# A two-layer hybrid trunk in split float32: 512-column moving operands in the second MLP, rotary tables and low parts moved to GpSimd in the first layer

## The chip, the core and the metric

The kernel runs on one core of a Trainium2 chip. The metric is device time in microseconds (us) of one execution. In the profile PE is TensorE (PEld its weight load), DVE is VectorE, ACT is ScalarE, POOL is GpSimd, and SP issues most of the DMAs. PEclk is the TensorE clock that was granted, as a share of full speed: 1.00 is 2.4 GHz, 0.50 is 1.2 GHz.

## The reference, cut to what matters

Sequence 256, model width 2048, 2 layers, all float32. The widths are: combined input projection 7184 columns, output projection 2048, MLP 8192. `adaLN` takes six vectors per layer from a product of the condition with a 2048 x 12288 matrix.

```python
cond = jax.nn.silu(c)
for layer in range(DEPTH):
    mod = (cond @ ada_w[layer] + ada_b[layer])[:, None, :]
    sh_a, sc_a, g_a, sh_m, sc_m, g_m = jnp.split(mod, N_MOD, axis=-1)
    h = rmsnorm(x, norm_mix_w[layer]) * (1.0 + sc_a) + sh_a
    x = x + g_a * hybrid_mixer(h, ..., w_in[layer], ..., w_out[layer])
    h = rmsnorm(x, norm_mlp_w[layer]) * (1.0 + sc_m) + sh_m
    x = x + g_m * (jnp.square(jax.nn.relu(h @ w_ff1[layer])) @ w_ff2[layer])
return rmsnorm(x, final_norm_w)
```

`hybrid_mixer` projects h, runs three mixers on column groups of the result (4 retention heads with rotary positions, 8 forgetting-attention heads, 4 mLSTM heads behind a short causal convolution), normalises each head, gates, and projects the concatenation with `w_out`.

## The kernel before

**Number format.** Every large product is done with both operands split into a high part (fp32r) and a low part (the fp32r rest). A weight block of 128 x 128 and an activation tile of 128 x 256 (features x positions) give three matmuls that add into the same PSUM region: high weight x low activation, low weight x high activation, high weight x high activation (`mm_b`, lines 253 to 255). Where the result is wanted with positions on the partitions, the activations are the stationary side and 512 weight columns move (`mm_a`, lines 264 to 266).

**Weights.** A chunk of 512 KB is loaded by SP into a `raw` buffer (6 of them), `split` (line 217) rounds it to the high part `wh` on ACT (line 222) and subtracts on DVE or POOL to get the low part `wl` (line 228). There are 3 buffers each of `wh` and `wl`. A chunk holds 8 blocks of 128 x 128: 2 tiles of the inner dimension x 512 columns. `pool_share` accumulates, and each time it reaches 1 the subtraction goes to POOL, else to DVE: in layer 0 it is 1.0 for the first groups of the input projection, 0.8 for the last, 0.5 for the two late blocks, 0.7 to 0.8 after that; in layer 1 it is 0.

**Order of a layer.** The input projection runs over 14 blocks of 512 columns (`BLOCKS`), in layer 0 in groups of the inner dimension (`win`, 2, 2, 2, 4 and 6 tiles of 128) because the adaLN vectors arrive in that order, with blocks `mo` and `rg` last; in layer 1 in one group. When a mixer's inputs are there, `mixers` (line 838) makes it a generator, and `tick` (line 826), called between chunks, advances up to two generators by one step. A step is a few small matmuls, the ACT and DVE work that follows, and a `yield`. Then comes `w_out`, which needs the mixers' outputs `Y`, then the MLP: `ff1` (line 965) and `ff2` (line 1002), in 8 stages of 1024 hidden features; `residual` (line 817) adds each `ff2` result to X with one DVE instruction per 128 x 256 tile (line 822). PSUM for all of these is `pj`: 2 buffers of 128 x 1024, each 4 output tiles.

**Lead.** Layer 1's input projection and both MLPs begin with `lead` (line 468): the first block is computed from X with the scale applied but without the row norm R, while R is still being worked out; `h_make` (line 510) then makes the normed h (`hh`, `hl`) for the rest, two tiles at a time: one DVE multiply (518), two ACT scalings (523), an ACT cast (525), a DVE subtraction (526).

**Adaptive vectors.** `ada` (line 269) streams the 2048 x 12288 matrices in 512 KB halves, reduced on DVE (line 284), spread over the whole program by `pump` and `rate`.

**Rotary tables.** `rope_tables` (line 176) computes cosine and sine of position x frequency with 20 small DVE instructions, most of them a range reduction, and three ACT ones. It is called from `late_constants` (line 153) after the third group of layer 0's input projection (`CONST_AT = 2`).

The Tile framework's scheduler, which simulates a timeline while it builds, fixes the order of instructions on each engine.

## Time and profile before

| | |
|---|---|
| median of 3 runs | 2540.33 us (2539.73 to 2541.04) |
| the profiled execution: its own time | 2544.26 us |
| its span, first to last instruction | 2542.5 us |
| PE busy | 2440.4 us |
| DVE, ACT, POOL busy | 1583.5, 1186.6, 758.0 us |
| mean granted TensorE clock | 0.982 |

How to read it: the span is the profiled execution's first to last instruction; the execution's own time is 1.8 us more. The matmuls are pipelined, so the duration of one (about 0.28 us) overlaps the next; how often they start is read by dividing a stretch by the number of them in it.

### The profile page before, as it was taken

Reading aid. Unit: us, or ns where it says so; the run is one execution under the profiler, and the core shown is the slowest. Engines: PE = TensorE matmul, PEld = TensorE weight load, DVE = VectorE, ACT = ScalarE, POOL = GpSimd, SP = SyncE. Lnnn points to the kernel's source line nnn. Section 1 sums busy time; section 2 is a strip of 40 time slices with the busy share of each in tenths; the row PEclk is TensorE's granted clock in tenths of the full one; section 3 lists DMA queues with packets and bytes.
Section 4 is the critical chain, followed back from the end, with each engine's and each line's share of the span. In section 5 each row is a group of like instructions: output and inputs, shape, how many; then the busy total and the mean of one; then the engine's idle time right before and its main releaser. Section 6 shows DMA issues by size and latency. Waiting matters only on the chain.

```text
span 2542.5 us, 46522 instructions
## 1 busy us (share of the span) xinstructions
PE 2440.4 (96%) x19016; PEld 2368.9 (93%) x19016; DVE 1583.5 (62%) x2426; ACT 1186.6 (47%) x1446; POOL 758.0 (30%) x315
## 2 busy tenths in 40 slices
PE   7999988888999999999999999999999999999997
PEld 6989977888999999999998999889999999999997
DVE  5787877677664544544388778556754554555554
ACT  4434454435543444444446456454644444344443
POOL 4867533344676666666500000000000000000000
PEclk8999999899999999999999999999999999999998
DMA  9988867589999988888667777555555555555552
GB/s 355 341 294 314 307 215 273 207 312 339 334 333 331 329 303 305 289 299 315 222 230 268 259 255 265 157 167 179 179 182 183 185 186 182 186 187 185 185 183 99
DMA packets 177247, 630.45 MB, mean 248 GB/s; under 512 B 19588, under 2 KB 24326, under 8 KB 177032
## 3 DMA queue, kind: packets, MB, share of 16 engines
q1 hardware_dynamic: 176600, 627.08, 70.9%
q8 instruction: 149, 2.44, 0.4%
q14 instruction: 66, 0.54, 0.1%
q10 hardware_dynamic: 432, 0.39, 0.1%
HBM read 625.30 MB, written 2.10 MB: 247 GB/s over the span
## 4 chain that ended last, share of the span: by engine, by line
PE 78%; DVE 7%; issue 5%; POOL 4%; DMA 4%; ACT 2%; SPq 0%; DVEq 0%; POOLq 0%; ACTq 0%
PE pj L254 22%; PE pj L253 22%; PE pj L255 22%; POOL wl L228 4%; DMA ada<-ada_w 3%; DVE wl L228 2%; PE pj L265 2%; PE pj L264 2%; PE pj L266 2%; DVE ada L284 1%; DMA raw<-w_in 1%; PE mx L646 1%; DVE blk L453 0%; PE mx L430 0%; DVE X L822 0%
## 5 line engine op out<-in xcount | busy, mean ns | idle before, releaser
L222 ACT CAST wh<-raw 128x1024 fp32r<-128x1024 f32 x804 | 840.5, 1047 | 1117.2 <-PE pj L255 898.6
L228 DVE TENSOR_TENSOR wl<-raw,wh 128x1024 fp32r<-128x1024 f32 x494 | 615.5, 1248 | 504.5 <-ACT wh L222 504.1
L228 POOL TENSOR_TENSOR wl<-raw,wh 128x1024 fp32r<-128x1024 f32 (+1 forms) x310 | 755.4, 2441 | 501.7 <-ACT wh L222 474.8
L253 PE MATMUL pj<-hl,wh 128*128 128x256 f32 x2912 | 828.7, 285 | 14.2 <-DVE hl L526 9.8
L254 PE MATMUL pj<-hh,wl 128*128 128x256 f32 x2912 | 829.2, 285 | 4.5 <-DVE wl L228 4.0
L255 PE MATMUL pj<-hh,wh 128*128 128x256 f32 x2912 | 826.9, 284 | 0.0
L254 PE MATMUL pj<-blk,wl 128*128 128x256 f32 x2528 | 713.8, 282 | 7.9 <-DVE wl L228 7.0
L253 PE MATMUL pj<-blk,wh 128*128 128x256 f32 x2528 | 711.6, 282 | 1.5 <-ACT blk L564 1.5
L255 PE MATMUL pj<-blk,wh 128*128 128x256 f32 x2528 | 711.8, 282 | 0.0
L253 PEld LDWEIGHTS pj<-hl,wh 128*128 128x128 f32 x2912 | 559.6, 192 | 16.4 <-DVE hl L526 10.5
L254 PEld LDWEIGHTS pj<-hh,wl 128*128 128x128 f32 x2912 | 560.1, 192 | 6.6 <-DVE wl L228 5.4
L255 PEld LDWEIGHTS pj<-hh,wh 128*128 128x128 f32 x2912 | 560.0, 192 | 0.2
L284 DVE SCALAR_TENSOR_TENSOR ada<-ada,cond 128x1024 f32<-128x1024 f32 x380 | 456.5, 1214 | 165.0 <-DMA ada<-ada_w 162.5
L254 PEld LDWEIGHTS pj<-blk,wl 128*128 128x128 f32 x2528 | 478.1, 189 | 9.0 <-DVE wl L228 7.6
L253 PEld LDWEIGHTS pj<-blk,wh 128*128 128x128 f32 x2528 | 478.5, 189 | 1.9 <-ACT blk L564 1.9
L255 PEld LDWEIGHTS pj<-blk,wh 128*128 128x128 f32 x2528 | 478.7, 189 | 0.1
L1075 POOL TENSOR_TENSOR blk<-blk,R 128x1024 f32<-128x1024 f32 x1 | 2.4, 2362 | 1276.2 <-ACT R L420 1276.2
L822 DVE SCALAR_TENSOR_TENSOR X<-pj,mod,X 128x256 f32<-128x256 f32 x284 | 117.9, 477 | 103.5 <-PE pj L255 103.3
L265 PE MATMUL pj<-wl,hh 128*128 128x512 f32 x384 | 154.0, 401 | 13.6 <-DVE wl L228 12.5
L264 PE MATMUL pj<-wh,hl 128*128 128x512 f32 x384 | 153.2, 399 | 1.0 <-ACT wh L222 1.0
L266 PE MATMUL pj<-wh,hh 128*128 128x512 f32 x384 | 152.0, 396 | 0.0
L265 PEld LDWEIGHTS pj<-wl,hh 128*128 128x128 f32 x384 | 73.2, 191 | 29.7 <-DVE wl L228 14.1
(232 smaller groups left out, 1642.5 us busy)
## 6 DMA issues: line engine op xcount, KB each, us to landing
raw<-w_ff SPq DMA_DIRECT2D x508, 512.0 KB, 4.0
ada<-ada_w SPq DMA_DIRECT2D x380, 512.0 KB, 6.4
raw<-w_in SPq DMA_DIRECT2D x224, 512.0 KB, 5.3
raw<-w_out SPq DMA_DIRECT2D x64, 512.0 KB, 4.4
X<-x SPq DMA_DIRECT2D x4, 512.0 KB, 7.1
raw<-ada_w SPq DMA_DIRECT2D x4, 512.0 KB, 9.8
raw<-w_ff SPq DMA_DIRECT2D x8, 256.0 KB, 3.3
out<-blk SPq DMA_DIRECT2D x4, 512.0 KB, 2.8
```

Source lines behind the costliest of these rows:

```text
L222: nc.scalar.copy(hi, raw)
L228: eng.tensor_tensor(lo, raw, hi.bitcast(F32), ALU.subtract)
L253: nc.tensor.matmul(o, lhsT=wh[:, s], rhs=al, start=st, stop=False, skip_group_check=True)
L254: nc.tensor.matmul(o, lhsT=wl[:, s], rhs=ah, start=False, stop=False, skip_group_check=True)
L255: nc.tensor.matmul(o, lhsT=wh[:, s], rhs=ah, start=False, stop=last, skip_group_check=True)
L264: nc.tensor.matmul(o, lhsT=al[:, s], rhs=wh, start=first, stop=False)
L265: nc.tensor.matmul(o, lhsT=ah[:, s], rhs=wl, start=False, stop=False)
L266: nc.tensor.matmul(o, lhsT=ah[:, s], rhs=wh, start=False, stop=last)
L284: nc.vector.scalar_tensor_tensor(raw, raw, 1.0, self.cond, ALU.mult, ALU.mult, accum_out=self.part[l][:, i, h:h + 1])
L646: nc.tensor.matmul(ps[:, i * P:i * P + P], lhsT=lt, rhs=v[:, j, c:c + P], start=first, stop=last, skip_group_check=True)
L822: V.scalar_tensor_tensor(self.X(k), ps[:, n * T:n * T + T], self.mod[l][:, c:c + 1], self.X(k), ALU.mult, ALU.add)
L1075: nc.gpsimd.tensor_tensor(o, o, self.R[:, None, :].to_broadcast((P, 4, T)), ALU.mult)
```

## The change

In layer 1's MLP the activation tiles lie as high part beside low part (one tile `h` in place of `hh` and `hl`), and `mm_w` does one matmul of 512 columns, high weight x [high | low], and one of 256, low weight x high. The two halves of the 512 columns land beside each other in PSUM and are added when they are read: `ff1_wide` by an ACT copy and a DVE add, `ff2_wide` by two DVE residual instructions per tile. A `pj` buffer holds 2 output tiles in place of 4, and a weight chunk is 4 inner tiles x 256 columns (`chunk2`), laid out so in memory. `square_wide` does the squared ReLU as one DVE instruction. The lead of that MLP keeps three matmuls per block, and takes its weights from two such chunks at a time (`lead_w2`). The last four output tiles (`ff2_tail`) are unchanged but for the layout.

In layer 1 a generator may take a step only on every second call of `tick` (`gap=2`). In layer 0 the rotary tables are computed on POOL at the start of the program, each fused multiply-add as two instructions (29 in place of 20 on DVE), with their two DMAs on ACT's queue; the other late constants come after the first group (`CONST_AT = 0`); all weight low parts up to `w_out` go to POOL; and the transposed attention probabilities are copied from PSUM by ACT in place of DVE.

```diff
-CFG = [dict(win=[2, 2, 2, 4, 6], late=2, lead_win=False, ada_win=[4, 4, 8, 12, 14], ada_late=4, ada_out=19,
+CFG = [dict(wide=False, gap=1, win=[2, 2, 2, 4, 6], late=2, lead_win=False, ada_win=[4, 4, 8, 12, 14], ada_late=4, ada_out=19,
             ff1=[8, 8], ff1_blocks=6, early_ff1=[[0, 1]], stat_ff1=(0, 1), ada_ff1=[16, 16], ada_ff=68,
-            pool_win=[1.0, 1.0, 1.0, 1.0, 0.8], pool_late=0.5, pool_out=0.7, pool_ff1=[0.7, 0.8], pool_ff=0.8),
-       dict(win=[16], late=0, lead_win=True, ada_win=[36], ada_late=0, ada_out=12, early_win=[[0, 1, 2], [], [3]],
+            pool_win=[1.0, 1.0, 1.0, 1.0, 1.0], pool_late=1.0, pool_out=0.7, pool_ff1=[0.7, 0.8], pool_ff=0.8),
+       dict(wide=True, gap=2, win=[16], late=0, lead_win=True, ada_win=[36], ada_late=0, ada_out=12, early_win=[[0, 1, 2], [], [3]],
             stat_win=(1, 2), ff1=[16], ff1_blocks=1, early_ff1=[[0, 1], [2], [], [], [3]], stat_ff1=(1, 2),
             ada_ff1=[4], ada_ff=12, pool_win=[0.0], pool_late=0.0, pool_out=0.0, pool_ff1=[0.0], pool_ff=0.0)]
...
-CONST_AT = 2
+CONST_AT = 0
...
-        self.hh = self.acts.tile([P, KT, T], F32R, name="hh")
-        self.hl = self.acts.tile([P, KT, T], F32R, name="hl")
+        self.h = self.acts.tile([P, KT, 2, T], F32R, name="h")
...
-            self.rope_tables()
...
+        m = self.tmp.tile([P, 2, T], F32, tag="ht", name="rm")[:, 0, :]
+        nc.scalar.dma_start(pi.bitcast(I32), self.io["positions"].partition_broadcast(P))
         rope = c.tile([P, 2], F32, name="rope")
-        nc.sync.dma_start(rope, self.io["rope"])
-        V = nc.vector
+        nc.scalar.dma_start(rope, self.io["rope"])
+        V = nc.gpsimd
...
             for cc in (c1, c2, c3):
                 for p in parts:
-                    V.scalar_tensor_tensor(a, p, -cc, a, ALU.mult, ALU.add)
+                    V.tensor_scalar(m, p, -cc, None, ALU.mult)
+                    V.tensor_tensor(a, m, a, ALU.add)
...
+    def chunk2(self, src):
+        raw = self.raw.tile([P, 4, 256], F32, tag="raw", name=self.name("raw"))
+        self.wdma.append(self.nc.sync.dma_start(raw, src))
+        hi, lo = self.split(raw, 4, 256)
+        return [(hi[:, i, :], lo[:, i, :]) for i in range(4)]
+    def mm_w(self, ps, w, act, first, last):
+        nc = self.nc
+        wh, wl = w
+        for n in range(2):
+            s = slice(n * P, n * P + P)
+            o = ps[:, n * 512:n * 512 + 512]
+            nc.tensor.matmul(o.rearrange("p (a b) -> p a b", b=T), lhsT=wh[:, s], rhs=act, start=first, stop=False,
+                             skip_group_check=True)
+            nc.tensor.matmul(o[:, :T], lhsT=wl[:, s], rhs=act[:, 0, :], start=False, stop=last, skip_group_check=True)
+    @staticmethod
+    def sums(ps):
+        v = ps.rearrange("p (n c) -> p n c", c=512)
+        return v[:, :, 0:T], v[:, :, T:2 * T]
 
...
-                (wh, wl), (uh, ul) = w[k - k0], self.U.pop(k)
+                uh, ul = self.U.pop(k)
                 f, e = k == kts[0], k == kts[-1]
                 for n in range(4):
-                    s = slice(n * P, n * P + P)
+                    wh, wl = w(k - k0, n)
                     o = ps[n][:, :LT]
-                    nc.tensor.matmul(o, lhsT=wh[:, s], rhs=ul, start=f, stop=False)
-                    nc.tensor.matmul(o, lhsT=wl[:, s], rhs=uh, start=False, stop=False)
-                    nc.tensor.matmul(o, lhsT=wh[:, s], rhs=uh, start=False, stop=e)
+                    nc.tensor.matmul(o, lhsT=wh, rhs=ul, start=f, stop=False)
+                    nc.tensor.matmul(o, lhsT=wl, rhs=uh, start=False, stop=False)
+                    nc.tensor.matmul(o, lhsT=wh, rhs=uh, start=False, stop=e)
...
+    def lead_w2(self, src):
+        def get(k, nk):
+            w = [self.chunk2(src[b, k // 4]) for b in range(2)]
+            return lambda i, n: tuple(x[:, n % 2 * P:n % 2 * P + P] for x in w[n // 2][i])
+        return get
 
...
-            nc.scalar.copy(self.hh[:, k:k + 2, :], t)
-            nc.vector.tensor_tensor(self.hl[:, k:k + 2, :], t, self.hh[:, k:k + 2, :].bitcast(F32), ALU.subtract)
+            hi, lo = self.h[:, k:k + 2, 0, :], self.h[:, k:k + 2, 1, :]
+            nc.scalar.copy(hi, t)
+            nc.vector.tensor_tensor(lo, t, hi.bitcast(F32), ALU.subtract)
 
...
-            V.tensor_copy(p, ps[:, 0:384])
+            (V.tensor_copy if l else nc.scalar.copy)(p, ps[:, 0:384])
...
+        self.ticks += 1
         n = 0
         for t in list(self.tasks):
             if n == LANES:
                 break
-            r = next(t, None)
+            if t[1] > self.ticks:
+                continue
+            r = next(t[0], None)
             if r is None:
                 self.tasks.remove(t)
-            else:
-                n += r
+            elif r:
+                n += 1
+                t[1] = self.ticks + self.gap
 
...
+                if cfg["wide"]:
+                    self.lead_out(ps, acc[0])
+                    acc[0] = self.square_wide(acc[0])
...
+    def ff1_wide(self, l, b, kts, acc=None):
+        nc = self.nc
+        done = kts[-1] == KT - 1
+        fresh = acc is None
+        t = self.slot() if fresh else acc
+        for h in range(2):
+            ps = self.pair()
+            for k0 in range(kts[0], kts[-1] + 1, 4):
+                w = self.chunk2(self.io["w_ff1_%d" % l][2 * b + h, k0 // 4])
+                for k in range(k0, k0 + 4):
+                    self.mm_w(ps, w[k - k0], self.h[:, k], k == kts[0], k == kts[-1])
+                self.step(0.5)
+            d = t[:, 2 * h:2 * h + 2, :]
+            p0, p1 = self.sums(ps)
+            if fresh:
+                nc.scalar.copy(d, p1)
+            else:
+                nc.vector.tensor_tensor(d, p1, d, ALU.add)
+            nc.vector.tensor_tensor(d, p0, d, ALU.add)
+        return self.square_wide(t) if done else t
+    def square_wide(self, t):
+        nc = self.nc
+        nc.vector.scalar_tensor_tensor(t, t, 0.0, t, ALU.max, ALU.mult)
+        out = []
+        for h in range(2):
+            s = self.slot((P, 2, 2, T), F32R)
+            nc.scalar.copy(s[:, 0], t[:, 2 * h:2 * h + 2, :])
+            nc.vector.tensor_tensor(s[:, 1], t[:, 2 * h:2 * h + 2, :], s[:, 0].bitcast(F32), ALU.subtract)
+            out.append(s)
+        return lambda i: out[i // 2][:, :, i % 2, :]
+    def ff2_wide(self, l, s, hid, last):
+        V = self.nc.vector
+        if last:
+            self.stat_begin()
+            self.per = 0.0
+        tail = last and l == DEPTH - 1
+        for nb in range(6 if tail else 8):
+            ps = self.pair()
+            for c in range(2):
+                w = self.chunk2(self.io["w_ff2_%d" % l][nb, 2 * s + c])
+                for i in range(4):
+                    self.mm_w(ps, w[i], hid[c](i), c == 0 and i == 0, c == 1 and i == 3)
+                self.step(0.5)
+            for n in range(2):
+                k = 2 * nb + n
+                g = self.mod[l][:, 5 * KT + k:5 * KT + k + 1]
+                with self.tc.high_priority(offset=URGENT * last):
+                    for c in range(n * 512, n * 512 + 512, T):
+                        V.scalar_tensor_tensor(self.X(k), ps[:, c:c + T], g, self.X(k), ALU.mult, ALU.add)
...
         self.constants()
+        self.rope_tables()
         self.stat_first()
...
+    for k in ("w_ff1", "w_ff2"):
+        for l in range(DEPTH):
+            a[f"{k}_{l}"] = _chunks(inp[k][l:l + 1], 256 if CFG[l]["wide"] else 512)[0]
```

**Order, first place.** PE near the end of layer 0's mixers; `mx` are the mixers' PSUM banks, `pj` the output projection, `pt` the decayed retention scores. Lines 635 and 636 (675 and 676 in the change) are the scores of one head, line 646 (686) their product with the values, which needs `pt` from DVE (L715, L716). Before:

```order
L254 MATMUL pj_4300<-blk_3619,wl_4379 128x256
L255 MATMUL pj_4300<-blk_3619,wh_4378 128x256
L635 MATMUL mx_3969<-blk_531,blk_564 128x256
L636 MATMUL mx_3969<-blk_531,blk_564 128x128
L646 MATMUL mx_3969<-blk_596,pt_3972 128x128 x3
L635 MATMUL mx_4015<-blk_531,blk_564 128x256
L636 MATMUL mx_4015<-blk_531,blk_564 128x128
L646 MATMUL mx_4015<-blk_596,pt_4018 128x128 x3
```

And in the change, for the head that corresponds to the first of these:

```order
L675 MATMUL mx_3978<-blk_569,blk_602 128x256
L676 MATMUL mx_3978<-blk_569,blk_602 128x128
L278 MATMUL pj_4309<-blk_3195,wh_4318 128x256
L279 MATMUL pj_4309<-blk_3194,wl_4319 128x256
L280 MATMUL pj_4309<-blk_3194,wh_4318 128x256
```

Before, a head's scores and its product stand side by side for three heads in a row; now 27 matmuls of `w_out` stand between the two.

**Order, second place.** DVE in the middle of layer 1's `ff2`. L822 (L1124 in the change) is the residual, which waits for the last matmul of its `pj` buffer and frees it; L228 the low part of a weight chunk. Before:

```order
L822 SCALAR_TENSOR_TENSOR X_91<-pj_22204,mod_127,X_91 128x256 x4
L228 TENSOR_TENSOR wl_22393<-raw_22390,wh_22392 128x1024
L228 TENSOR_TENSOR wl_22399<-raw_22396,wh_22398 128x1024
L228 TENSOR_TENSOR wl_22458<-raw_22455,wh_22457 128x1024
L228 TENSOR_TENSOR wl_22464<-raw_22461,wh_22463 128x1024
L822 SCALAR_TENSOR_TENSOR X_92<-pj_22329,mod_127,X_92 128x256 x4
```

And in the change:

```order
L1124 SCALAR_TENSOR_TENSOR X_91<-pj_20098,mod_126,X_91 128x256 x3
L228 TENSOR_TENSOR wl_20200<-raw_20197,wh_20199 128x1024
L1124 SCALAR_TENSOR_TENSOR X_91<-pj_20098,mod_126,X_91 128x256
L228 TENSOR_TENSOR wl_20222<-raw_20219,wh_20221 128x1024
L1124 SCALAR_TENSOR_TENSOR X_92<-pj_20147,mod_126,X_92 128x256 x3
L228 TENSOR_TENSOR wl_20249<-raw_20246,wh_20248 128x1024
L1124 SCALAR_TENSOR_TENSOR X_92<-pj_20147,mod_126,X_92 128x256
```

Four residual instructions came with every four low parts, and now come with every two. The low parts between them belong to the buffer after the next one.

**Order, third place.** POOL at the start of the program; `rt` and `rm` are the rotary tables' scratch tiles. Before, after its set-up:

```order
L228 ISA
L228 TENSOR_TENSOR wl_214<-raw_211,wh_213 128x1024
L228 TENSOR_TENSOR wl_247<-raw_244,wh_246 128x1024
L228 TENSOR_TENSOR wl_280<-raw_277,wh_279 128x1024
L228 TENSOR_TENSOR wl_307<-raw_304,wh_306 128x1024
```

And in the change, where 15 rotary instructions stand ahead of this piece:

```order
L202 TENSOR_TENSOR rt<-rm,rt 128x256
L201 TENSOR_SCALAR rm<-rt 128x256
L228 TENSOR_TENSOR wl_252<-raw_249,wh_251 128x1024
L202 TENSOR_TENSOR rt<-rm,rt 128x256
L228 TENSOR_TENSOR wl_285<-raw_282,wh_284 128x1024
L228 TENSOR_TENSOR wl_318<-raw_315,wh_317 128x1024
L192 TENSOR_SCALAR rt<-rt 128x256
L193 TENSOR_SCALAR rt<-rt 128x256
```

The first low part is now behind 17 rotary instructions, the fourth behind 25.

## Rows read from the trace of the kernel before

**Rows 1.** The page: busy time of each engine, and the chain that ended last.

```profile
PE 2440.4 (96%) x19016; PEld 2368.9 (93%) x19016; DVE 1583.5 (62%) x2426; ACT 1186.6 (47%) x1446; POOL 758.0 (30%) x315
...
PE 78%; DVE 7%; issue 5%; POOL 4%; DMA 4%; ACT 2%; SPq 0%; DVEq 0%; POOLq 0%; ACTq 0%
```

**Rows 2.** Windows: stretch and its length, then busy time (instructions) of each engine.

```profile
core 0: us, PE busy (x) PEld busy (x) DVE busy (x) ACT busy (x) POOL busy (x), PEclk, DMA share, GB/s
...
1900.00:2500.00 600.00, 600.00 (x5047) 600.00 (x5046) 317.09 (x340) 256.33 (x252) 0.00 (x0) 1.00 0.56 185
...
1614.00:1640.00 26.00, 26.00 (x116) 21.51 (x115) 11.19 (x13) 16.37 (x22) 0.00 (x0) 1.00 0.61 183
...
137.00:177.00 40.00, 33.69 (x228) 30.97 (x227) 37.63 (x51) 13.79 (x18) 24.03 (x11) 0.96 0.73 245
...
340.00:470.00 130.00, 104.27 (x562) 88.43 (x561) 89.91 (x204) 66.23 (x114) 36.28 (x15) 0.88 0.59 211
...
413.40:423.60 10.20, 6.62 (x22) 5.27 (x20) 10.20 (x12) 2.95 (x4) 2.97 (x1) 0.50 0.51 161
447.50:468.00 20.50, 12.71 (x53) 11.14 (x52) 10.75 (x56) 11.48 (x25) 0.00 (x0) 0.50 0.00 0
```

**Rows 3.** Waits of PE from 340 to 470 us: total us, times, longest.

```profile
PE pj L265 <- DVE wl L228: 9.2, 4, 3.6
PE mx L646 <- DVE pt L716: 4.7, 3, 2.9
PE mx L807 <- DVE blk L799: 4.6, 1, 4.6
...
PE pj L253 <- ACT blk L564: 1.5, 1, 1.5
```

**Rows 4.** Groups of instructions from 1840 to 2500 us (layer 1's MLP), DVE and ACT.

```profile
L228 DVE TENSOR_TENSOR wl<-raw,wh 128x1024 fp32r<-128x1024 f32 x232 | 284.0, 1224 | 297.5 <-ACT wh L222 297.5
...
L822 DVE SCALAR_TENSOR_TENSOR X<-pj,mod,X 128x256 f32<-128x256 f32 x120 | 49.8, 478 | 15.8 <-PE pj L255 15.8
...
L222 ACT CAST wh<-raw 128x1024 fp32r<-128x1024 f32 x231 | 242.2, 1048 | 349.1 <-PE pj L255 337.9 <-DVE wl L228 10.7 <-ACT wh L222 0.5
```

**Rows 5.** Timeline of DVE at a residual: start, us, instruction, idle before and releaser.

```profile
1785.88 1.66 DVE L822 SCALAR_TENSOR_TENSOR X<-pj,mod,X 128x256 f32<-128x256 f32 x4 [0.56 <-PE pj L255]
```

**Rows 6.** Groups on ACT, 1803 to 1831 us, and PE's wait there (from 1700).

```profile
L523 ACT ACTIVATE ht<-ht,mod 128x256 f32<-128x256 f32 x16 | 8.7, 593 | 1.6 <-DVE ht L518 1.6
L525 ACT CAST hh<-ht 128x512 fp32r<-128x512 f32 x8 | 4.9, 615 | 0.1
...
PE pj L253 <- DVE hl L526: 1.4, 1, 1.4
```

**Rows 7.** One rotary line on DVE (ns min/median/max), and PE's waits, 137 to 180 us.

```profile
L193 DVE TENSOR_SCALAR rt<-rt x2: 293/1043/1793, 141.5 to 158.0; 128x256 f32<-128x256 f32 x2
...
PE mx L294 <- DVE ada L284: 2.6, 2, 2.1
PE pj L253 <- DVE blk L567: 2.3, 1, 2.3
```

**Rows 8.** Groups from 340 to 470 us (low parts), and the convolution's line over the program.

```profile
L228 POOL TENSOR_TENSOR wl<-raw,wh 128x1024 fp32r<-128x1024 f32 x15 | 38.0, 2535 | 94.7 <-ACT wh L222 94.7
...
L228 DVE TENSOR_TENSOR wl<-raw,wh 128x1024 fp32r<-128x1024 f32 x11 | 20.2, 1845 | 0.5 <-ACT wh L222 0.5
...
L735 DVE SCALAR_TENSOR_TENSOR cv<-blk,vec,cv x48: 433/478/2701, 299.2 to 1574.6; 128x255 f32<-128x255 f32 x16, 128x254 f32<-128x254 f32 x16, 128x253 f32<-128x253 f32 x16
```

**Rows 9.** Waits of PE in layer 1's input projection, 1380 to 1700 us.

```profile
PE pj L265 <- DVE wl L228: 3.2, 1, 3.2
PE mx L646 <- DVE pt L687: 1.5, 1, 1.5
```

**Rows 10.** Timeline at the start: POOL's first low part, PE's first weight matmul.

```profile
24.04 2.35 POOL L228 TENSOR_TENSOR wl<-raw,wh 128x1024 fp32r<-128x1024 f32 x1 [23.60 <-ACT wh L222]
...
32.18 0.58 PE L253 MATMUL pj<-hl,wh 128*128 128x256 f32 x1 [6.67 <-DVE hl L526]
```

More of the change, by code (lines that the diff above doesn't have):

```diff
@@ L479, in lead @@
             nk = min(4, kts[-1] + 1 - k0)
-            w = self.chunk(wsrc(k0, nk), nk)
+            w = wsrc(k0, nk)
             for k in range(k0, k0 + nk):
@@ L496, in lead, with lead_w, get @@
         return ps
+    def lead_w(self, src):
+        def get(k, nk):
+            w = self.chunk(src[0, k // 4][:, k % 4:k % 4 + nk, :], nk)
+            return lambda i, n: tuple(x[:, n * P:n * P + P] for x in w[i])
+        return get
+    def lead_w2(self, src):
+        def get(k, nk):
+            w = [self.chunk2(src[b, k // 4]) for b in range(2)]
+            return lambda i, n: tuple(x[:, n % 2 * P:n % 2 * P + P] for x in w[n // 2][i])
+        return get
     def lead_out(self, ps, dst, func=AF.Identity, scale=1.0):
@@ L842, in mixers @@
             g = int(nm[2])
[L843 removed]
+            self.tasks.append([self.fox(l, B.pop("fq%d" % g), B.pop("fk%d" % g), B.pop("fv%d" % g), g), 0])
         elif nm == "mq":
@@ L862, in layer @@
         io = self.io
-        self.state, self.Y, self.tasks = {}, {}, []
+        self.state, self.Y, self.tasks, self.ticks, self.gap = {}, {}, [], 0, cfg["gap"]
         G = self.groups(cfg["win"])
@@ L870, in layer @@
             if led:
-                ps = self.lead(l, 0, 1, lambda k, n: io["w_in"][l, 0, k // 4][:, k % 4:k % 4 + n, :], kts, cfg["stat_win"])
+                ps = self.lead(l, 0, 1, self.lead_w(io["w_in"][l]), kts, cfg["stat_win"])
             if l > 0:
@@ L930, in layer @@
         NST = 8
+        ff1, ff2 = (self.ff1_wide, self.ff2_wide) if cfg["wide"] else (self.ff1, self.ff2)
         hid = [None] * NST
@@ L940, in layer @@
             if led:
-                ps = self.lead(l, 3, 4, lambda k, n: io["w_ff1"][l, 0, k // 4][:, k % 4:k % 4 + n, :], kts, cfg["stat_ff1"])
+                ps = self.lead(l, 3, 4, (self.lead_w2 if cfg["wide"] else self.lead_w)(io["w_ff1_%d" % l]), kts, cfg["stat_ff1"])
             self.h_make(l, 3, 4, kts)
@@ L950, in layer @@
             for b in range(1 if led else 0, nb):
-                acc[b] = self.ff1(l, b, kts, acc.get(b))
+                acc[b] = ff1(l, b, kts, acc.get(b))
         self.pool_share = cfg["pool_ff"]
@@ L955, in layer @@
             if s < NST:
-                hid[s] = [acc.pop(2 * s + i) if 2 * s + i < nb else self.ff1(l, 2 * s + i, list(range(KT)))
+                hid[s] = [acc.pop(2 * s + i) if 2 * s + i < nb else ff1(l, 2 * s + i, list(range(KT)))
                           for i in range(2)]
@@ L959, in layer @@
                 self.pump_until(l, 5, KT - 1)
-                self.ff2(l, s - 1, hid[s - 1], s == NST)
+                ff2(l, s - 1, hid[s - 1], s == NST)
                 hid[s - 1] = None
@@ L970, in ff1 @@
             r0 = k0 % 4
-            w = self.chunk(self.io["w_ff1"][l, b, k0 // 4][:, r0:r0 + nk, :], nk)
+            w = self.chunk(self.io["w_ff1_%d" % l][b, k0 // 4][:, r0:r0 + nk, :], nk)
             for i in range(nk):
@@ L1006, in ff2 @@
             self.per = 0.0
-        tail = last and l == DEPTH - 1
-        for nb in range(3 if tail else 4):
+        for nb in range(4):
             ps = self.pair()
@@ L1012, in ff2 @@
                     self.early(CFG[l + 1]["early_win"], c, l + 1, 0, 1)
-                w = self.chunk(self.io["w_ff2"][l, nb, 2 * s + c], 4)
+                w = self.chunk(self.io["w_ff2_%d" % l][nb, 2 * s + c], 4)
                 hi, lo = hid[c]
@@ new lines, in square_wide @@
+    def square_wide(self, t):
[27 more added lines that the diff above has]
+                        V.scalar_tensor_tensor(self.X(k), ps[:, c:c + T], g, self.X(k), ALU.mult, ALU.add)
+            if last and nb % 2 == 1:
+                self.stat_piece(nb // 2)
@@ L1024, in ff2 @@
             if tail:
-                for n in range(4):
-                    self.final_scale(4 * nb + n)
+                for n in range(2):
+                    self.final_scale(2 * nb + n)
         if tail:
@@ L1113, in _layout @@
     a["w_gate"] = np.ascontiguousarray(g.reshape(DEPTH, KT, P, NG).transpose(0, 2, 1, 3))
-    for k in ("w_out", "w_ff1", "w_ff2"):
-        a[k] = _chunks(inp[k])
+    a["w_out"] = _chunks(inp["w_out"])
+    for k in ("w_ff1", "w_ff2"):
+        for l in range(DEPTH):
+            a[f"{k}_{l}"] = _chunks(inp[k][l:l + 1], 256 if CFG[l]["wide"] else 512)[0]
     vec = np.zeros((P, DEPTH * NVEC + KT), np.float32)
```

24 lines of the change are left out of this document (11 added, 13 removed).

## The prediction, made before the change was run

> **What bounds the kernel now.** I read the page first [rows 1]: PE is busy 96% of the span and carries 78% of the chain that ended last, while DVE is at 62%. So only two things shorten the program: PE doing its work in fewer or shorter intervals, and the 4% in which PE waits or its clock is low. I then went through windows [rows 2]. Most of the MLPs look like 1900 to 2500 us: PE is never idle and the clock is at 1.00. What PE loses sits in a few stretches of layer 0: 137 to 177 us has 40 − 33.7 = 6.3 us idle, 340 to 470 us has 130 − 104.3 = 25.7 us idle, and there the clock falls to 0.50 (1.2 GHz) for 10.2 + 20.5 us, each time after PE had waited. PE's waits in that last stretch name DVE: low parts that come late, then the retention scores and head gates [rows 3].
>
> **1. 512-column operands.** In 600 us stand 5047 matmuls of 256 columns, some two of them begun earlier [rows 2]: 600 / 5045 = 118.9 ns from one to the next, 356.8 ns for the three of a weight block. In 26 us stand 116 of 512 columns, some 1.5 begun earlier: 227 ns, not 2 x 118.9 = 238. A matmul thus costs some 11 ns whatever its width. A block in the change takes 227 + 118.9 = 345.9 ns, 10.9 less. It does so for 1952 blocks: ff1 has 15 blocks of 64 outside the lead (960), ff2 8 stages of 128 less the 32 of the tail (992). That is 1952 x 10.9 = 21 us, all on the path, since PE has no idle time there. No row shows a 512 followed by a 256 of the same region; the ends are 0 (a 512 costs as two 256s) and 27 us (26 / 116 = 224 ns); I take 21, because the neighbours on both sides were measured.
> The Trainium skill ("TensorE: Matmul & The Clock Gate", § Back-to-back issue gap) gives an isolated gap of N / 2.4 + 2.5 ns, so about 109 ns for 256 columns and 216 for 512. By it, as an estimate, a block would gain only 2.5 ns, and the change 1952 x 2.5 = 5 us. The trace has 118.9 and 227 in their place.
>
> **2. The load beside it.** Per ff2 buffer PE now has 16 blocks, 16 x 345.9 = 5.5 us (11.4 before). DVE has two low parts and four residuals: 2 x 1.224 + 4 x 0.478 = 4.4 us [rows 4]. It starts 0.56 us after the last matmul [rows 5], and by its order (second place) has freed the buffer after 3 + 1 residuals and one low part, 0.56 + 1.91 + 1.22 = 3.7 us, against 5.5 us until PE wants it. ACT needs 2 x 1.048 us. Cost nothing; the slack is 1.8 us. The DMA rate rises from 185 to some 190 GB/s, under the 245 of another window [rows 2]: nothing. The extra adds of ff1 have 11 us per buffer: nothing. The new layouts and the fused tile move no work: nothing.
>
> **3. Entry into that MLP.** The lead now takes two chunks at once, of three buffers; the second of the next pair can be cast only when the first of the old pair is done, and PE reaches it about a microsecond too early. Three such borders, between 0 and 3 x (1.05 + 1.22) = 6.8 us [rows 4]; I take 3, since half of each is covered by the last blocks of the old pair. Then the first ff1 buffer runs through all 16 tiles of h in 32 x 0.346 = 11.1 us, where it took 64 x 0.357 = 22.8 us. ACT needs 16 x 0.593 + 8 x 0.615 = 14.4 us for h [rows 6], and 4 casts more, 18.6 us. PE waits 1.4 us there already. Between 0 (h made ahead) and 18.6 − 11.1 = 7.5 us; I take 3, as the scheduler puts blocks of the second buffer between. Together +6.
>
> **4. Rotary tables off DVE.** From 137 to 177 us DVE is busy 37.6 of 40 us [rows 2], and a rotary instruction takes 0.29 us alone but 1.79 us where it overlaps a POOL low part [rows 7]. PE waits 2.6 us on late adaptive vectors and 2.3 on a late PSUM read. Of 6.3 us idle and 1.6 us of lost clock (0.04 x 40) I take back 6; ends 0 and 8.
>
> **5. Low parts to POOL.** In layer 0's mixers DVE's 11 low parts take 1.845 us in place of 1.224, and PE waits 9.2 us for them [rows 3, 8]. POOL takes 2.5 us each; in the late blocks a chunk is 12 matmuls of 512 columns, 12 x 0.227 = 2.7 us of PE, plus the mixers' own: POOL keeps up, barely. I take back 8; the ends are 9 gained, and 9 lost where POOL is late as often as DVE was.
>
> **6. The mixers' tail.** The retention steps now have 27 matmuls, 3.2 us, between scores and product (first place), more than the longest such wait, 2.9 us. The waits for `pt` 4.7, for the gates 4.6 and for ACT 1.5 [rows 3] make 10.8 us; I take back 5 (0 to 11), since the chain of norm and gate stays. Of 30.7 us at half clock PE worked 19.3 [rows 2]; full clock would give half, 9.7 us. I take 3 (0 to 9), as the tail keeps some waits. The copies moved from DVE to ACT are inside this term.
>
> **7. Steps two calls apart in layer 1.** Only 1.5 us of waits there are a mixer's own, 3.2 a low part's [rows 9]. I take back 1; ends 4 gained, 4 lost if retention is late for w_out.
>
> **8. The start.** POOL has nothing to do until 24 us, PE no weight matmul until 32.2 us [rows 10], which waits on DVE. No row shows a rotary instruction on POOL. A quarter of a low part, 0.6 us, makes 17 x 0.6 = 10 us, done in time; a whole 2.4 us each makes 41 us, and with the wait for the positions PE is up to 20 us late. The quarter is nearer, by its size. Cost +1 (0 to 20).
>
> Sum: −21 + 6 − 6 − 8 − 5 − 3 − 1 + 1 = −37 us. The profiled execution's 2544.26 us becomes 2507; it lies 3.9 us above the median of 2540.33, so the median becomes **2503 us**. A measurement of this kernel tells 0.2%, some 5 us, from no change.
>
> **The rivals.**
> A. Wide operands save little (term 1 between 0 and 10, say 5). For it: no row shows the mixed sequence. Against: the 227 and 118.9 ns. 2503 + 16 = 2519. Chance 0.10.
> B. Layer 0 gives nothing: terms 5 and 6 vanish, because POOL is busier and DVE's instructions with two SBUF inputs wait for it. For it: a convolution step takes 2.7 us against 0.43, a low part on DVE 1.845 against 1.224 [rows 4, 8]. There are 24 such steps. Against: DVE loses more work than it waits. 2503 + 16 + 3 for new collisions = 2522. Chance 0.16. The Trainium skill ("SBUF — State Buffer") calls the pair of ports that DVE and GpSimd share an exclusive lock, held for the whole instruction; the trace agrees, with 1.79 against 0.29 us.
> C. Slower: in ff2 DVE does not empty a buffer in time, so each of 62 buffers (8 x 8 − 2) waits. Its work per buffer is 4.4 us and it decides beyond 5.5, so where residuals take 0.76 us in place of 0.478. To eat 37 us and 5 more it must reach 5.5 + 42 / 62 = 6.2 us. Then 2546. Against: the slack of term 2. Chance 0.04.
> D. The waits of 340 to 470 us vanish almost wholly (low parts, tail and clock at their good ends): 9 + 11 + 9 in place of 16, so 2503 − 13 = 2490. Chance 0.10.
>
> **How the numbers follow.** The forecast has 0.60, the rivals 0.10, 0.16, 0.04 and 0.10. The range 2485 to 2527 takes in A, B and D with a few us of their own, and leaves out C, a start that is 20 us late, and the far sides of A, B and D, less than 2 in 10. Faster by over 0.2%: all but C and the part of B with several terms at their bad ends, 0.92; within 0.2%: 0.04; slower: 0.04.
>
> **What would show it.** In the changed profile: 600 / 345.9 x 2 = some 3470 matmuls in 600 us of that MLP with PE still at 100%; PE waits of about 6 us around its entry, on h and on low parts; no rotary line and no wait on `ada` between 137 and 177 us; no wait of PE on DVE's `wl` in layer 0's mixers, and fewer than 30 us at half clock there; PE's first weight matmul still near 32 us. The prediction is wrong if PE has idle time inside ff2, if POOL's `wl` heads the waits, or if the 512 + 256 pair takes over 352 ns.

## The result, and the profile after

The changed kernel takes 2510.05 us (median of 4 runs, 2507.29 to 2516.56) beside 2540.68 us for the kernel before on the same chip: a ratio of 0.9884, 95% interval 0.9864 to 0.9903. A second measurement (change_again, below) gave 2508.85 us beside 2535.78, a ratio of 0.9894 (0.9879 to 0.9909). So the change is 27 to 31 us faster; 37 were forecast. The profiled execution took 2509.01 us (span 2506.9), 35.3 us less than the profiled one before, which lies 3.6 us above the median of its kernel; so stretches that are compared between the two profiles add up to more than the medians differ by.

The page, as in [rows 1]: PE is now busy 97% of the span with fewer, longer matmuls, and POOL has taken work over from DVE. DVE is nevertheless busier than before, 65% in place of 62%, because of the extra additions and residuals.

```profile
PE 2422.3 (97%) x17064; PEld 2267.9 (90%) x17064; DVE 1634.7 (65%) x2568; ACT 1178.9 (47%) x1469; POOL 822.5 (33%) x360
...
PE 72%; DVE 5%; DMA 3%; issue 1%; ACT 0%; SPq 0%; DVEq 0%; ACTq 0%
```

To see where the time came from I cut the span at five instructions that both programs have, read from the timeline: the first weight matmul, the first matmul of layer 0's MLP lead, of layer 1's first lead, of layer 1's MLP lead, and of the tail (the last four output tiles). Stretches in us:

| | start | layer 0, mixers and w_out | layer 0, MLP | layer 1, mixers and w_out | layer 1, MLP | tail | span |
|---|---|---|---|---|---|---|---|
| before | 32.2 | 524.0 | 754.6 | 475.0 | 720.6 | 36.1 | 2542.5 |
| change | 32.8 | 495.2 | 752.8 | 477.6 | 711.5 | 37.0 | 2506.9 |
| forecast of the difference | +1 | −22 | 0 | −1 | −15 | 0 | −37 |

Four fifths of the gain are in layer 0's mixers, more than forecast; the MLP of layer 1 gives 9 where 15 were forecast. The last of these borders does not stand behind the same work in both programs: before, 23 matmuls of `ff2` (2.8 us) follow the tail's first matmul, in the change none. With all of `ff2` counted to the MLP in both, the MLP gives 9.1 + 2.8 = 11.9 us, and what follows `ff2`'s last matmul takes 37.0 us in place of 33.3. One of PE's waits in the tail has doubled; here it is before, then in the change:

```profile
PE mx L390 <- DVE ss L382: 1.9, 1, 1.9
PE mx L415 <- DVE ss L407: 3.8, 1, 3.8
```

Together, the MLP and the tail give 8.2 us.

The windows that answer to [rows 2]. The last one holds as many matmuls as 340 to 470 us did, counted from the program's start, though in another order:

```profile
core 0: us, PE busy (x) PEld busy (x) DVE busy (x) ACT busy (x) POOL busy (x), PEclk, DMA share, GB/s
...
1860.00:2460.00 600.00, 600.00 (x3436) 525.36 (x3435) 404.54 (x517) 255.46 (x272) 0.00 (x0) 1.00 0.61 188
...
137.00:177.00 40.00, 40.00 (x287) 37.77 (x286) 25.98 (x38) 16.43 (x18) 32.04 (x15) 1.00 0.95 338
...
336.00:436.00 100.00, 94.04 (x563) 82.11 (x562) 71.89 (x179) 56.63 (x94) 58.64 (x24) 0.98 0.79 279
```

In these 600 us of the MLP PE has no idle time at all, and they hold 3436 matmuls: with two of them begun earlier, as in the prediction, 600 / 1717 = 349.4 ns for a pair of 512 and 256 columns, where the three of 256 took 356.8. From 137 to 177 us PE is never idle (6.3 us before). The mixers' last stretch has shrunk from 130 to 100 us: PE idles 100 − 94.04 = 6.0 us where it was 25.7, at a mean clock of 0.98 instead of 0.88.

PE's waits in the whole of layer 0's mixers and `w_out`, 34 to 528 us, beside [rows 3]. From 336 to 436 us only the third, the fourth and the last of these stand, so no low part is left there. Over the whole, POOL's low parts now head the list, and DVE's come second, in `w_out`.

```profile
PE pj L279 <- POOL wl L228: 4.3, 3, 2.0
PE pj L279 <- DVE wl L228: 2.4, 2, 2.2
PE mx L686 <- DVE pt L756: 2.3, 1, 2.3
PE mx L665 <- DVE blk L852: 2.2, 1, 2.2
PE mx L686 <- ACT pt L727: 2.2, 1, 2.2
PE mx L847 <- DVE blk L839: 1.8, 1, 1.8
PE pj L278 <- ACT blk L604: 1.5, 1, 1.5
```

DVE in ff2 of layer 1, which answers to [rows 4, 5] (start, us, instruction, idle before): a buffer every 5.60 us, the first residual 0.62 us after the last matmul, three residuals, a low part, the fourth residual. The buffer is free 2.93 us after DVE took it up and PE wants it 2 us later. The group's row shows 480 ns for a residual over all 239.

```profile
2240.54 1.40 DVE L1124 SCALAR_TENSOR_TENSOR X<-pj,mod,X 128x256 f32<-128x256 f32 x3 [0.62 <-PE pj L262]
2241.85 1.22 DVE L228 TENSOR_TENSOR wl<-raw,wh 128x1024 fp32r<-128x1024 f32 x1
2242.99 0.48 DVE L1124 SCALAR_TENSOR_TENSOR X<-pj,mod,X 128x256 f32<-128x256 f32 x1
2244.30 1.23 DVE L228 TENSOR_TENSOR wl<-raw,wh 128x1024 fp32r<-128x1024 f32 x1 [0.83 <-ACT wh L222]
2246.14 1.40 DVE L1124 SCALAR_TENSOR_TENSOR X<-pj,mod,X 128x256 f32<-128x256 f32 x3 [0.62 <-PE pj L262]
```

PE's waits at the entry of that MLP, 1740 to 1800 us, beside the 1.4 us of [rows 6]; the second stands ahead of the lead:

```profile
PE pj L260 <- DVE h L566: 3.0, 3, 1.2
PE pj L279 <- DVE wl L228: 0.6, 1, 0.6
```

The rotary tables on POOL, in the first 60 us (groups of instructions), and PE's first weight matmul, which answers to [rows 10]. All 29 rotary instructions there add up to 21.9 us, between POOL's low parts:

```profile
L201 POOL TENSOR_SCALAR rm<-rt 128x256 f32<-128x256 f32 x9 | 7.6, 850 | 0.8
L202 POOL TENSOR_TENSOR rt<-rm,rt 128x256 f32<-128x256 f32 x9 | 6.6, 731 | 0.6
```

```profile
32.81 0.58 PE L278 MATMUL pj<-h,wh 128*128 128x256 f32 x1 [6.09 <-DVE h L566]
```

### The profile page after: what moved, and what is told of

Read it like the earlier page. It is cut to its first block, busy times and chain, and to the rows that moved or that the text cites. A ratio compares the mean times of both kernels' runs of the same rounds, so it can differ in the third digit from the quotient of the medians.

```text
span 2506.9 us, 42898 instructions
## 1 busy us (share of the span) xinstructions
PE 2422.3 (97%) x17064; PEld 2267.9 (90%) x17064; DVE 1634.7 (65%) x2568; ACT 1178.9 (47%) x1469; POOL 822.5 (33%) x360
## 4 chain that ended last, share of the span: by engine, by line
PE 72%; DVE 5%; DMA 3%; issue 1%; ACT 0%; SPq 0%; DVEq 0%; ACTq 0%
PE pj L260 18%; PE pj L279 12%; PE pj L278 12%; PE pj L280 12%; PE pj L262 9%; DMA ada<-ada_w 2%; DVE wl L228 2%; PE pj L290 1%; PE pj L289 1%; PE pj L291 1%; DVE ada L309 1%; PE mx L686 0%; DVE blk L478 0%; PE mx L515 0%; DVE h L566 0%
## 5 line engine op out<-in xcount | busy, mean ns | idle before, releaser
L228 POOL TENSOR_TENSOR wl<-raw,wh 128x1024 fp32r<-128x1024 f32 (+1 forms) x326 | 798.2, 2453 | 396.7 <-ACT wh L222 385.6
L228 DVE TENSOR_TENSOR wl<-raw,wh 128x1024 fp32r<-128x1024 f32 x478 | 587.3, 1230 | 387.7 <-ACT wh L222 386.7
L279 PE MATMUL pj<-h,wl 128*128 128x256 f32 x1952 | 559.0, 287 | 7.5 <-DVE wl L228 4.2
L278 PE MATMUL pj<-h,wh 128*128 128x256 f32 x1952 | 557.5, 286 | 7.8 <-DVE h L566 6.9
L280 PE MATMUL pj<-h,wh 128*128 128x256 f32 x1952 | 555.7, 285 | 0.0
L278 PE MATMUL pj<-blk,wh 128*128 128x256 f32 x1536 | 434.8, 283 | 2.9 <-ACT blk L604 1.5
L280 PE MATMUL pj<-blk,wh 128*128 128x256 f32 x1536 | 433.9, 283 | 0.0
L279 PEld LDWEIGHTS pj<-h,wl 128*128 128x128 f32 x1952 | 376.9, 193 | 10.4 <-DVE wl L228 5.5
L278 PEld LDWEIGHTS pj<-h,wh 128*128 128x128 f32 x1952 | 376.2, 193 | 8.7 <-DVE h L566 7.1
L280 PEld LDWEIGHTS pj<-h,wh 128*128 128x128 f32 x1952 | 376.7, 193 | 0.2
L260 PE MATMUL pj<-blk,wh 128*128 128x512 f32 x992 | 347.4, 394 | 0.0
L260 PE MATMUL pj<-h,wh 128*128 128x512 f32 x960 | 336.7, 395 | 3.1 <-DVE h L566 3.0
L279 PEld LDWEIGHTS pj<-blk,wl 128*128 128x128 f32 x1536 | 292.5, 190 | 5.9 <-DVE wl L228 3.6
L278 PEld LDWEIGHTS pj<-blk,wh 128*128 128x128 f32 x1536 | 292.8, 191 | 3.7 <-ACT blk L604 1.7
L280 PEld LDWEIGHTS pj<-blk,wh 128*128 128x128 f32 x1536 | 292.6, 191 | 0.0
L262 PE MATMUL pj<-h,wl 128*128 128x256 f32 x960 | 268.9, 280 | 0.0
L260 PEld LDWEIGHTS pj<-blk,wh 128*128 128x128 f32 x992 | 186.2, 188 | 43.2
```

The costliest lines, as they stand in the source:

```text
L228: eng.tensor_tensor(lo, raw, hi.bitcast(F32), ALU.subtract)
L260: nc.tensor.matmul(o.rearrange("p (a b) -> p a b", b=T), lhsT=wh[:, s], rhs=act, start=first, stop=False, skip_group_check=True)
L262: nc.tensor.matmul(o[:, :T], lhsT=wl[:, s], rhs=act[:, 0, :], start=False, stop=last, skip_group_check=True)
L278: nc.tensor.matmul(o, lhsT=wh[:, s], rhs=al, start=st, stop=False, skip_group_check=True)
L279: nc.tensor.matmul(o, lhsT=wl[:, s], rhs=ah, start=False, stop=False, skip_group_check=True)
L280: nc.tensor.matmul(o, lhsT=wh[:, s], rhs=ah, start=False, stop=last, skip_group_check=True)
```

## The experiments

Each was measured in five rounds beside the kernel before. The change itself stands at 0.9884 and 0.9894. The stretch of layer 0's mixers, from the first weight matmul to the MLP's lead, is the measure for its parts. It differs between executions: five profiles of a program with the change's layer 0 gave 495.2, 497.2, 497.9, 500.6 and 503.1 us. A sixth, wide_both, in which every engine runs this stretch in the change's order too, gave 507.0.

**no_wide: the MLP of layer 1 as before.**

```diff
-       dict(wide=True, gap=2, win=[16], ...
+       dict(wide=False, gap=2, win=[16], ...
```

> Layer 1's MLP as before (256-column operands, 512-column weight chunks, lead on one chunk), everything else as in the change. By the prediction's terms 1 and 3 (-21 and +6) it should take 15 us more than the change, about 2525. By the interval that the changed trace shows (600 us hold 3436 matmuls, so 349.3 ns for a pair where 345.9 was forecast, 14.5 us in all) less an entry that costs 6, it is 9 us more, 2519, and the stretch from the MLP's lead to its tail takes 720 us as before instead of 711. Rival: DVE's extra residuals take back what PE gains, then it is the change's own time, 2510 give or take 3.

Measured: 2515.74 us, ratio 0.9919 (0.9906 to 0.9931), and the MLP's stretch 720.8 us, against 711.5. The second of the three expectations holds for the stretch; by the time it is some 7 us. The two agree once the border is set right: here too 23 matmuls of `ff2` stand behind the tail's first, so the wide operands with their entry give 9.3 + 2.8 = 12.1 us in the MLP. The tail behind `ff2`'s last matmul takes 32.3 us here and 37.0 in the change, where PE waits 3.8 us on `ss` in place of 1.9. That leaves 7. The window of the same length shows three matmuls of 256 again:

```profile
1860.00:2460.00 600.00, 600.00 (x5045) 600.00 (x5045) 316.24 (x336) 254.65 (x248) 0.00 (x0) 1.00 0.55 185
```

**pair_order: what a pair costs.** Both 512-column matmuls of a column pair first, then both of 256 (in outline):

```diff
-        for n in range(2):
-            matmul(512 columns, wh of n); matmul(256 columns, wl of n)
+        for n in range(2): matmul(512 columns, wh of n)
+        for n in range(2): matmul(256 columns, wl of n)
```

> The same four matmuls of two weight blocks, but both 512-column ones first, then both 256-column ones, so that no 256-column one follows the 512-column one whose columns it adds to. In the changed trace a 512-column matmul is followed after 232 us/1000 and a 256-column one after 116 to 118, 349.3 ns the pair, where 227 + 118.9 was forecast. If the extra 5 ns is the cost of coming back to the same columns, the pair falls to 346 and the time by 1952 x 3.4 = 6.6 us, 600 us then hold some 3470 matmuls. If each width simply costs what it costs, 349 ns stay and the time is the change's. Third: two 256-column ones in a row cost more than one behind a 512, since less time hides the weights of the next; then over 350 ns and up to 4 us slower.

Measured: 2509.89 us, 0.9897 (0.9883 to 0.9910), the change's own time, and 3437 matmuls in the window:

```profile
1860.00:2460.00 600.00, 600.00 (x3437) 523.92 (x3436) 404.85 (x515) 255.18 (x273) 0.00 (x0) 1.00 0.61 189
```

The starts of the matmuls in the trace say the same by width (medians): behind a 512 comes the next after 232 to 233 ns, be it a 512 or a 256, and behind a 256 after 115 to 119, whichever follows. Coming back to the same columns costs nothing here; a 512-column matmul takes 232 ns, and 227 in the stretch of [rows 2] where the weights are the moving operand. Why they differ no run tells.

**gap1: layer 1's steps on consecutive calls.**

```diff
-       dict(wide=True, gap=2, win=[16], ...
+       dict(wide=True, gap=1, win=[16], ...
```

> Layer 1's mixer steps on consecutive calls again, two at a time, the rest as in the change. Term 7 says 1 us more than the change, with 4 either way; on this chip the change stands near 0.988 of the kernel before. The stretch from layer 1's first lead to its second took 475.0 us before and 471.4 to 477.6 in the five traces with steps two calls apart, so the step itself is not seen against that spread unless the stretch leaves it, say 480 or more. Rival: spacing the steps is what keeps the waits of PE on low parts and norms there small; then 480 to 485 and a ratio near 0.991.

Measured: 2511.4 us, 0.9904 (0.9890 to 0.9917), overlapping the change's interval. Layer 1's mixers took 476.0 us, within the 471.4 to 477.6 of the change and its first four variants, and before 475.0. Spacing the steps does nothing that can be told there.

**rope_dve and low_dve: one part of layer 0 undone at a time.** In the first, the rotary tables are worked out on DVE behind the third group, with their old loads and instructions; in the second:

```diff
-            pool_win=[1.0, 1.0, 1.0, 1.0, 1.0], pool_late=1.0, ...
+            pool_win=[1.0, 1.0, 1.0, 1.0, 0.8], pool_late=0.5, ...
```

> The rotary tables back on DVE, behind the third group of the first layer's projections, their loads and the other late constants with them; the rest as in the change. Term 4 says 6 us more than the change (less 1 for the start), about 2515, with PE idle again for 4 to 6 us where the tables are worked out, and single rotary instructions of 1.8 us wherever they meet a POOL low part. Rival: since the last groups' low parts have left DVE, it has room for the tables, and the time stays at 2510 give or take 3. Third: the gain near 137 to 177 us was not the tables but the late loads that went with them; then PE's wait there is on something else than DVE.

> Low parts of the last group at a share of 0.8 on GpSimd and of the late blocks at 0.5, as before; the rest as in the change. Term 5 says 8 us more than the change, about 2518, with PE waiting some 9 us for DVE's low parts between the fifth group and w_out and the clock at half for longer. Rival B's core: POOL's low parts slow DVE by as much as they relieve it, then 2510 give or take 3. If the new steps two calls apart alone cleared that stretch, PE's waits there stay below 3 us on low parts.

Measured: rope_dve 2519.93 us, 0.9936 (0.9924 to 0.9948), stretch 509.2; low_dve 2519.73 us, 0.9935 (0.9922 to 0.9948), stretch 507.6. Each costs 11 us against the 2508.85 of the change. The stretches alone could not show it, since 507.0 was also reached with nothing undone; the waits do. In the first the window of 137 to 177 us is again that of [rows 2] but for the last digits, with some 8 us of idle time and lost clock:

```profile
137.00:177.00 40.00, 33.68 (x229) 30.96 (x228) 37.63 (x51) 13.97 (x18) 24.02 (x11) 0.96 0.74 249
```

In the second PE's waits on DVE's low parts are back, 12.1 us from 350 to 560 us where the change has 2.4:

```profile
PE pj L290 <- DVE wl L228: 7.5, 4, 3.5
PE pj L279 <- DVE wl L228: 4.6, 1, 4.6
```

**pt_dve, and again: the copy of the softmax weights back on DVE.**

```diff
-            (V.tensor_copy if l else nc.scalar.copy)(p, ps[:, 0:384])
+            V.tensor_copy(p, ps[:, 0:384])
```

> The copy of the transposed softmax weights of layer 0 back on DVE, the rest as in the change. It is a part of term 6 (5 us) that was not priced alone: 8 copies of three 128 x 128 blocks. If DVE's queue is what the mixers wait for, 2 to 5 us more than the change, 2512 to 2515. If the gain of the tail comes from the low parts alone, 2510 give or take 2.

> The change with the copy of layer 0's softmax weights back on DVE, a second time and on this chip. If its gain is a real one the ratio is again 0.984 to 0.987, and the stretch to the MLP's lead is near 491 where five traces of the same layer 0 with the copy on ACT show 495 to 503. If it was scatter, 0.988 to 0.991.

Measured: 2501.03 us, 0.9856 (0.9844 to 0.9869), and 2499.49 us, 0.9849 (0.9836 to 0.9863); the stretch 491.4 and 491.5. Neither expectation for the first had a gain: this part of the change costs some 8 us. The copy itself is no slower on ACT (479 ns in the middle, 552 on DVE). The edit also changes the order in which the scheduler sets the other instructions, and no run holds that order still.

**pt_only: the other two undone, the copy on ACT.** The edits of rope_dve and low_dve together.

> Rotary tables back on DVE and the low parts at their former shares, both at once; the copy of the softmax weights stays on ACT in layer 0, and layer 1 is the change's. What is left of the change in layer 0 is that copy alone. If the parts add up, the time is the change plus 11 plus 11, 2531, a ratio near 0.998. If the copy costs some 8 us in any state, layer 0 is worse than in the kernel before: its stretch from the first weight matmul to the MLP's lead 524 + 8 = 532, the ratio over 1.000. If the copy helps where DVE is behind and hurts only where DVE has been relieved, that stretch is below 524, about 516, and the ratio near 0.994.

Measured: 2519.53 us, 0.9929 (0.9916 to 0.9942), stretch 509.6. The last of the three comes nearest: with the copy on ACT alone the mixers take 524.0 − 509.6 = 14.4 us less than in the one profile of the kernel before; by the times it is some 12, that is 19.2 us less 7 for layer 1's MLP. Once tables and low parts are gone from DVE the same copy adds some 8 (4 to 16 by the stretches). And with the copy on ACT, undoing both other parts costs no more than undoing either (509.6 beside 509.2 and 507.6). A reading that fits is that the parts replace each other, since each takes work from DVE, and the stretch is short only when enough of it is gone. It is argued, not shown: each edit also brings another order of the instructions.

**ada_early: what the copy on ACT costs, and where.** The loss is not at the softmax but in w_out: counted by matmuls, the change is level with pt_dve at 473 us, and some 5 us behind it at the MLP's lead. Three windows of 440 to 530 us, of the change, of pt_dve and of this experiment:

```profile
440.00:530.00 90.00, 82.35 (x644) 81.10 (x643) 64.33 (x103) 36.01 (x46) 42.96 (x19) 0.92 0.84 302
```

```profile
440.00:530.00 90.00, 87.37 (x735) 86.75 (x734) 66.37 (x115) 41.87 (x56) 48.56 (x20) 1.00 0.85 315
```

```profile
440.00:530.00 90.00, 86.22 (x712) 85.42 (x710) 57.49 (x101) 40.52 (x53) 49.65 (x20) 0.98 0.82 293
```

In the change PE idles 7.65 us there at a mean clock of 0.92, with the copy on DVE 2.63 at 1.00. DVE's timeline in the change shows a candidate: an adaptive product waits 8.10 us for its weights, and the residual of a finished w_out block stands behind it.

```profile
500.65 1.22 DVE L309 SCALAR_TENSOR_TENSOR ada<-ada,cond 128x1024 f32<-128x1024 f32 x1 [8.10 <-DMA ada<-ada_w]
501.80 0.08 DVE L309 DVE_READ_ACCUMULATOR ada<-ada,cond 128x1 f32 x1
501.80 1.66 DVE L862 SCALAR_TENSOR_TENSOR X<-pj,mod,X 128x256 f32<-128x256 f32 x4
503.37 1.21 DVE L228 TENSOR_TENSOR wl<-raw,wh 128x1024 fp32r<-128x1024 f32 x1
```

Where the products stand on DVE is the scheduler's choice, and it differs between the two programs. So four tiles of them were moved ahead:

```diff
-            ... ada_late=4, ada_out=19,
+            ... ada_late=8, ada_out=15,
```

> The change with layer 0's adaptive products moved: 8 instead of 4 tiles in the late blocks, 15 instead of 19 during w_out; the copy of the softmax weights stays on ACT. In the change DVE waits 17 to 18 us between 440 and 530 us for loads of adaptive weights, once 8.1 us with a finished w_out residual behind it, and ACT, PE and the clock follow; with the copy on DVE that wait is 7.4 to 8.4 us and the time 8 us less. If this wait is what the copy on ACT costs, the stretch to the MLP's lead falls from 495 to 503 to some 491, the ratio to 0.985 to 0.987. If the products only wait elsewhere, or are in DVE's way in the late blocks, the stretch stays at 495 or more and the ratio at 0.989.

Measured: 2499.09 us, 0.9858 (0.9828 to 0.9887), stretch 493.4, idle in the window 3.78 us. As fast as pt_dve by the median, though the interval overlaps the change's. Its stretch is only 1.8 us below the change's first one, less than that stretch differs between executions. And DVE's wait on those loads is still 14.4 us there (the first line is the change's, then pt_dve's, then this one's), so the wait by itself is not what was taken away:

```profile
DVE ada L309 <- DMA ada<-ada_w: 18.0, 4, 8.1
```

```profile
DVE ada L309 <- DMA ada<-ada_w: 7.4, 4, 2.8
```

```profile
DVE ada L309 <- DMA ada<-ada_w: 14.4, 6, 7.4
```

Shown is where the change falls behind pt_dve, and that PE idles less there when the products stand elsewhere. That their order is the cause, or this residual's wait, is argued only.

**wide_both: layer 0's MLP wide too.** The flag set for both layers; the early pieces of layer 1's lead moved to the last two of eight column pairs.

> Layer 0's MLP with 512-column operands too, the rest as in the change. If the saving of layer 1 holds there, 960 blocks at 11 ns and 1024 at 6 give 16.7 us, less some 3 for entries, so 10 to 14 us below the change, a ratio near 0.983, and the stretch from layer 0's second lead to layer 1's first falls from 753 to some 740 us. Rival: layer 0 still works out adaptive vectors (152 of 1.2 us in 650 us of DVE) and its POOL holds up DVE, so half-size buffers are not emptied in 5.5 us and PE waits on residuals; then no gain, or slower, with PE's waits there named by X or by a PSUM buffer.

Measured: 2531.24 us, 0.9976 (0.9966 to 0.9986), 22 us slower than the change beside it (change_again); layer 0's MLP took 762.9 us, and 15 more of its matmuls (2.6 us) stand behind the border, so it lost some 13. PE's waits there, 560 to 1300 us:

```profile
PE pj L260 <- DVE X L1128: 10.5, 4, 7.1
PE pj L260 <- DVE blk L1092: 7.6, 4, 4.5
```

This is rival C's mechanism, in the layer where DVE also has the adaptive products (155 of 1.2 us) and POOL is at work: half-size buffers that DVE doesn't empty in time. Layer 1's mixers lost nothing: their 479.4 us hold those 2.6. Layer 0's took 507.0, in the same order of instructions as the change's 495.2 to 503.1; so some 9 of the 22 us have no cause that was found.

**best: the copy on DVE, and only layer 0's ten undivided ff1 blocks wide.** ff1 takes its wide form for blocks 6 to 15 of layer 0, with a second layout of those weights.

> The copy back on DVE, and in layer 0 the ten ff1 blocks that run over all 16 tiles at once take 512-column operands (ff2 and the six split blocks stay as they are). 640 weight blocks at 360 less 348.9 ns give 7 us, a ratio near 0.983, and the stretch of layer 0's MLP falls from 755 to 748. Rival: DVE's extra work there (additions of the two halves, the squares) delays its low parts and residuals as in the run with both MLPs wide, where PE waited 18 us on residuals and half sums; then 755 or more and no gain. Between them: ff1 alone gives no wait on X, since the waits on X belong to the half buffers of ff2.

Measured: 2502.76 us, 0.9854 (0.9841 to 0.9868). The MLP's stretch fell to 749.4 us (752.0 and 755.5 in pt_dve) and PE has no wait on X; layer 1's mixers took 479.6 where pt_dve had 472 to 475. No gain that can be told from pt_dve. **change_again**, the change beside these runs:

> The change itself beside these, for their common scale: a ratio of 0.9864 to 0.9903, as first measured, and a stretch between layer 1's leads within 471 to 478 us, which says how much of that stretch differs from run to run with the same program.

It measured the 0.9894 above, with stretches of 497.2 and, for layer 1's mixers, 474.9 us: those differ by 2 to 3 us between executions of one program.

## Why the prediction was right

The time lies 7 us above the forecast, inside its range. That the total came so near is in part luck: layer 0 gave more than forecast and layer 1 less. The steps went as follows.

1. **512-column operands: right in kind, too large.** A block takes 349.4 ns where 345.9 was worked out: −14.5 us instead of −21. The sum 227 + 118.9 failed in its first member, a 512-column matmul taken from another stretch; here it takes 232 (pair_order). Its bound of 0 to 27 held the value, and the sign that would have refuted it (over 352 ns) did not come. Before, the blocks took 360 ns in ff1 and 354 in ff2, by the starts of consecutive matmuls; now 349 and 350. So ff1 gains 11 ns a block and ff2 only 4, and "some 11 ns whatever its width" does not hold: in ff2 two matmuls of 256 columns cost only 2 × 118 − 232 = 4 ns more than one of 512. By the rule on the back-to-back issue gap that the prediction weighed (the Trainium skill, "TensorE: Matmul & The Clock Gate") it would, as an estimate, have been 5 us; the trace lies between.
2. **The load beside it: right.** PE idles 0 us in 600; DVE's order at a buffer is the one read from the program, done with 2 us to spare. wide_both shows what happens without that slack.
3. **Entry into the MLP, and the tail: too large, and put at nothing.** On equal matmuls the MLP's 11.9 us are some 14.5 by the blocks less 2.6 for the rest, where +6 was forecast. The three lead borders cost nothing: from its first to its last matmul the lead takes 24.2 us, 24.1 before. The late `h` costs 3.0 us, 1.6 more than before; 1 us lies beside it, unnamed. The tail was taken with "The new layouts and the fused tile move no work: nothing", and it costs 3.7 us more. The wait on `ss` is 1.9 of them; why it has doubled stays open.
4. **Rotary tables: right.** 6.3 us of idle time and the 1.6 us of lost clock are gone from 137 to 177 us, 7.9 in all where 6 (0 to 8) was forecast; no rotary line is left there. In rope_dve both are back.
5. and 6. **Low parts and the mixers' tail: right together, wrong apart.** By the two profiles the stretch lost 28.8 us where terms 4 to 6 said 22; with the other executions of the same layer 0 it would be 17 to 29. But "The copies moved from DVE to ACT are inside this term" hid a part with a sign of its own: −12 to −14 us alone, some +8 beside the others (pt_dve, pt_only). And the terms were added as if each took its own waits away; with the copy on ACT undoing one or two of them costs the same 11 us. POOL nearly kept up: PE waits 4.3 us for its low parts. By the letter the sign "if POOL's `wl` heads the waits" has come, but the list that it heads has shrunk; DVE's low parts alone took 9.2 us before. The 100 us from 336 to 436 have a mean clock of 0.98, so some 4 us at half clock where it was 30.7.
7. **Steps two calls apart: no effect**, within the −1 (±4) forecast.
8. **The start: right**, 0.6 us. The 17 rotary instructions ahead of POOL's first low part took 0.77 us each where 0.6 was worked out. They began only at 11.15 us, after the positions' load, and the first low part at 26.68 us, 2.6 later than before, which PE did not have to wait for. All 29 take 22 us of POOL; the tables are first read at 374 us.

Not forecast are 1.8 us in layer 0's MLP, of the size by which executions differ, and the tail's 3.7. Of the rivals, A has not come, though term 1's 14.5 us lie between its 5 and the 21. B's outcome is refuted by layer 0's 28.8 us and by low_dve. C is shown in the layer where it was not asked for. D lies as far off as the forecast: less the 7.9 of term 4, the stretch lost 20.9 us, between the forecast's 16 and D's 29. The forecast's own sum was nearly reached by luck: layer 0 gave 30.6 us with its MLP where 22 were forecast, and layer 1 with the tail 5.6 where 16 were.
